# Attention in a streaming encoder step: the sink as one more column of the exponential, and the division by the sums placed behind the other unit's split

## The chip, the cores and the metric

The kernel is one program for one core of a Trainium2 chip. A NeuronCore has five engines that run their own instruction streams in order: TensorE (PE: matmuls, with the weight loads drawn as a row of their own, PEld), VectorE (DVE), ScalarE (ACT), GpSimd (POOL) and SyncE (SP, which only issues DMAs here). The metric is the device time of one launch, in microseconds; a comparison uses the median of several runs.

## The reference, cut to what matters

The reference is one inference step of an encoder with two layers: a recurrent layer (RG-LRU), then shared keys and values, then a layer of sliding-window attention with 16 heads in 4 groups, each group sharing one key/value head. 1024 prompt rows and 32 sample rows go through it. The change concerns the softmax, which has one learnt number per head, the sink, as an extra candidate that takes weight and gives no value:

```python
def sink_softmax(s, sink):
    m = jnp.maximum(jnp.max(s, axis=-1, keepdims=True), sink)
    p = jnp.exp(s - m)
    return p / (jnp.sum(p, axis=-1, keepdims=True) + jnp.exp(sink - m))
...
    p = sink_softmax(s, sink)
    o = jnp.einsum('bnkgqs,bnskd->bnqkgd', p.astype(vb.dtype), vb)
```

A block of 128 query rows sees at most 256 keys: its own block and the one before, masked in chunks of 64.

## The kernel before

The recurrent layer, the key/value projections and the queries of group 0 fill the first part of the program (lines 92 to 987). Every fp32 product is made of three matmuls: a helper `split` (lines 112 to 117) rounds an operand to a high half on ScalarE (L116) and subtracts to get the low half on VectorE (L117), and TensorE multiplies high by high, high by low and low by high.

The attention is the loop at lines 1058 to 1076. It runs over four groups g and, in each, over nine units j: eight blocks of 128 prompt rows and one of the sample rows, 36 units in all. A unit has three stages:

- `stage_s` (lines 903 to 941): the scores S of four heads (one for the sample unit) by two matmuls each (L925) into PSUM banks that are two deep; on VectorE one fused instruction per head adds the mask, scales, writes the negated scores into the unit's tile P and gives the row's extreme against the negated sink into `sm` (L927, followed by a read of the accumulator); on ScalarE the exponential of each head in place, with the row sum as a second result (L930). Then the sink's share: VectorE adds sink and extreme (L932), ScalarE takes the exponential of those four numbers (L933), VectorE adds it to the sums (L934) and takes the reciprocal (L935). Last the division: heads 2 and 3 on ScalarE (L938), heads 0 and 1 on VectorE (L940). P is two deep.
- `stage_t` (lines 943 to 952): TensorE transposes the powers of each of the (up to) two key blocks into PSUM banks T, two deep (L949), and `split` makes the halves ph on ScalarE and pl on VectorE.
- `stage_o` (lines 954 to 968): the output matmuls with ph and pl against the packed values (L959) into a single PSUM bank O, which ScalarE and VectorE then empty (L961, L967).

The loop issues the scores of unit j+1 first, then the transposes and split of unit j, then some steps of `fillers` (other matmuls that need no attention result: the gate projection `gB`, the next group's query projection `rAq`/`rBq`, and in the last group the first output projection `obm`), then the output matmuls of unit j. So a unit's transposes stand one round behind its scores, with the fillers between.

What is written so is not yet the order on the engines. The framework's scheduler reorders the instructions of each engine by a timeline that it simulates itself; `urgent()` raises the priority of what stands inside it, and `pin(i)` (line 79) keeps an instruction behind what the program issues ahead of it. All engines then run the order in which the scheduler left them. Lines 824 to 827 load the sinks into a tile `snk` and make their negatives `nsnk`.

Of the kernel before, what the change touches and what calls it, by code (L numbers as in the profile page):

```python
# [9 lines left out]
F32 = mybir.dt.float32  # L10
F32R = mybir.dt.float32r
AF = mybir.ActivationFunctionType
ALU = mybir.AluOpType
# [4 lines left out]
P = 128  # L18
# [45 lines left out]
def _trunk(ctx, tc, nc, A):  # L64
    V, S, G = nc.vector, nc.scalar, nc.gpsimd
# [13 lines left out]
    def pin(i, on=True):  # L79
        return tc.keep_in_program_order(i) if on else i  # L80

    def bank(name, tag="mm", bufs=None):
        return psum.tile([P, 512], F32, tag=tag, name=name, bufs=bufs or nbank)
# [28 lines left out]
    def split(dst_hi, dst_lo, src, lo_eng=None, hi_dve=False, behind=False):  # L112
        if hi_dve:
            V.tensor_copy(dst_hi, src)
        else:
            pin(S.activation(dst_hi, src, AF.Copy), behind)  # L116
        (lo_eng or V).tensor_tensor(dst_lo, src, dst_hi.bitcast(F32), op=ALU.subtract)  # L117
# [444 lines left out]
    for n in range(3):  # L562
        for m in LATE:
            w = NSB[n][1] - NSB[n][0]
# [87 lines left out]
    for n, order in enumerate(orders):  # L652
        zs, acc = {}, []
        w = NSB[n][1] - NSB[n][0]
# [25 lines left out]
    def att_tile(name, shape, dt, tag, bufs):  # L680
        return att.tile([P] + shape, dt, tag=tag, bufs=bufs, name=name)

    def kv_tile(name, shape, dt, tag, bufs=1):
        return kvp.tile([P] + shape, dt, tag=tag, bufs=bufs, name=name)
# [38 lines left out]
    def run(gen):  # L723
        for _ in gen:
            pass
# [95 lines left out]
    smask = kv_tile("smask", [256], F32, "smask")  # L821
    V.memset(smask, 0.0)
    V.memset(smask[:, 160:], NEG)
    snk = kv_tile("snk", [20], F32, "snk")
    nsnk = kv_tile("nsnk", [20], F32, "nsnk")
    nc.scalar.dma_start(snk, A["snk"])
    V.tensor_scalar(nsnk, snk, -1.0, None, op0=ALU.mult)

    prep_v()
    for n in range(3):  # L830
# [37 lines left out]
    ON_ACT = (2, 3)  # L868
# [5 lines left out]
    def load_kv(g, n):  # L874
        KU[g, n] = att_tile(f"K{g}_{n}", [2, 640], F32R, "K", 2)
        VU[g, n] = att_tile(f"V{g}_{n}", [5, 128], F32R, "V", 2)
        w = KB1[n] - KB0[n]
        for dup in range(2):
            for half in range(2):
                p0 = dup * 64 + half * 32  # L880
                pin(nc.sync.dma_start(KU[g, n][p0:p0 + 32, :, :w].bitcast(F32),
                                      kscr.rearrange("(l f) p c -> p l f c", l=2)[32 * g:32 * g + 32, :, half, KB0[n]:KB1[n]]),
                    g == 0 and n > 0)
        t0, t1 = KB0[n] // P, KB1[n] // P
        nc.sync.dma_start(VU[g, n][:, :t1 - t0, :].bitcast(F32),
                            vscr.rearrange("t p c -> p t c")[:, t0:t1, g * 128:g * 128 + 128])
# [16 lines left out]
    def stage_s(g, j):  # L903

        smp = j == 8
        n = 2 if smp else j // 3
        if (g, n) not in KU:
            load_kv(g, n)
        nm = f"{g}_{j}"
        nh, nk = (1 if smp else 4), (1 if j == 0 else 2)  # L910
        t0 = 3 if smp else max(j - 1, 0) - KB0[n] // P
        w = nk * P
        ks = slice(t0 * P, t0 * P + 256)
        sm = att_tile(f"sm{nm}", [4, 4], F32, "sm", 4)
        nmax, d, rsum, rl = (sm[:, i, :nh] for i in range(4))
        sk = slice(16 + g, 17 + g) if smp else slice(4 * g, 4 * g + 4)
        msk = smask if smp else mask[:, 256 - w:]
        pt = att_tile(f"P{nm}", [4, 256], F32, "P", 2)
        for h0 in range(0, nh, 2):
            sb = bank(f"S{nm}_{h0}", "S", 2)  # L920
            for h in range(h0, min(h0 + 2, nh)):
                q = QS[g].rearrange("p h c -> p (h c)") if smp else QU[g, n][:, h, P * j - NSB[n][0]:P * j - NSB[n][0] + P]
                s = sb[:, (h - h0) * 256:(h - h0) * 256 + 256]
                for hl in range(2):
                    pin(nc.tensor.matmul(s, q, KU[g, n][:, hl, ks], start=hl == 0, stop=hl == 1), g == 0 and j == 0)  # L925
            for h in range(h0, min(h0 + 2, nh)):
                V.tensor_tensor_reduce(pt[:, h, :w], sb[:, (h - h0) * 256:(h - h0) * 256 + w], msk,  # L927
                                       -0.125, nsnk[:, sk][:, h:h + 1], op0=ALU.add, op1=ALU.min,
                                       accum_out=nmax[:, h:h + 1])
                S.activation(pt[:, h, :w], pt[:, h, :w], AF.Exp, bias=nmax[:, h:h + 1], scale=-1.0,  # L930
                             accum_out=rsum[:, h:h + 1])
        V.tensor_tensor(d, snk[:, sk], nmax, op=ALU.add)  # L932
        S.activation(d, d, AF.Exp)  # L933
        V.tensor_tensor(rsum, rsum, d, op=ALU.add)  # L934
        V.reciprocal(rl, rsum)  # L935
        for h in range(nh):
            if h in ON_ACT:
                S.activation(pt[:, h, :w], pt[:, h, :w], AF.Copy, scale=rl[:, h:h + 1])  # L938
            else:
                V.tensor_scalar(pt[:, h, :w], pt[:, h, :w], rl[:, h:h + 1], None, op0=ALU.mult)  # L940
        return dict(P=pt, nh=nh, nk=nk, t0=t0, n=n, nm=nm, smp=smp)

    def stage_t(st):
        nm, w = st["nm"], st["nh"] * P
        st["p"] = []
        for kt in range(st["nk"]):
            tb = bank(f"T{nm}_{kt}", "T", 2)[:, :w]
            for h in range(st["nh"]):
                nc.tensor.transpose(tb[:, h * P:(h + 1) * P], st["P"][:, h, kt * P:(kt + 1) * P], ident)  # L949
            hl = [att_tile(f"p{x}{nm}_{kt}", [512], F32R, "p" + x, 2)[:, :w] for x in "hl"]  # L950
            split(*hl, tb)
            st["p"].append(hl)

    def stage_o(g, j, st):
        n, w, nk = st["n"], st["nh"] * P, st["nk"]
        ob = bank(f"O{st['nm']}", "O", 1)[:, :w]
        for kt in range(nk):
            for i, x in enumerate(st["p"][kt]):
                nc.tensor.matmul(ob, VU[g, n][:, st["t0"] + kt, :], x, start=kt + i == 0, stop=kt == nk - 1 and i == 1)  # L959
        half = kv_tile(f"oh{st['nm']}", [512], F32, "oh")  # L960
        S.activation(half[:64, :w], ob[64:128], AF.Copy)  # L961
        q = w // 4
        c0 = 256 if st["smp"] else P * j - NSB[n][0]
        if (g, n) not in TT:
            TT[g, n] = [unit(f"T{g}_{n}_{i}", w=NSB[n][1] - NSB[n][0]) for i in range(2)]
        for h in range(4):
            V.tensor_tensor(TT[g, n][h // 2][64 * (h % 2):64 * (h % 2) + 64, c0:c0 + q],  # L967
                            ob[:64, h * q:(h + 1) * q], half[:64, h * q:(h + 1) * q], op=ALU.add)
# [3 lines left out]
    def finish_og(g, n):  # L972
        for i in range(2):
            t, m = TT[g, n][i], 2 * g + i
            V.scalar_tensor_tensor(t, t, 0.5, SG.pop((m, n)), op0=ALU.mult, op1=ALU.mult)
            if g < 3:
                nc.scalar.dma_start(ogscr[m][:, NSB[n][0]:NSB[n][1]], t)
            else:
                ogl[m, n] = t
        del TT[g, n]  # L980
# [8 lines left out]
    def fillers(g):  # L989
        for m in (2 * g, 2 * g + 1):  # L990
            prep_m(f"g{m}", A["w_in_b"][8 + m], KD, 3)
        for n in range(3):
            for m in (2 * g, 2 * g + 1):
                yield from gate_block(m, n)
            if g == 3:
                for m in OG_AT[n]:
                    load_og(m, 0)
        for m in (2 * g, 2 * g + 1):
            del wts[f"g{m}"]
        if g < 3:  # L1000
            for x, nm in enumerate("AB"):
                prep_m(f"q{nm}{g + 1}", A["w_in_b"][2 * (g + 1) + x], KD, 3)
            for n in range(3):
                yield from q_block(g + 1, n)
        else:
            yield from out_b(0)
# [51 lines left out]
    for g in range(4):  # L1058
        fil = fillers(g)
        per = PER[g]  # L1060
        todo = [0, 1, 2]
        st = {0: stage_s(g, 0)}
        for j in range(9):
            if j < 8:
                st[j + 1] = stage_s(g, j + 1)
            stage_t(st[j])
            for _ in range(per - (g == 3 and j > 6)):
                next(fil, None)
            stage_o(g, j, st.pop(j))
            while todo and j >= (2, 5, 8)[todo[0]] and (2 * g + 1, todo[0]) in SG:  # L1070
                finish_og(g, todo.pop(0))
        if g == 3:
            break
        run(fil)
        for n in todo:
            finish_og(g, n)
# [164 lines left out]
```

## Time and profile before

| what | before |
|---|---|
| median of the timed runs | 914.59 us (914.43, 914.59, 915.57) |
| the profiled execution, its own time | 918.22 us |
| its span, first to last instruction | 916.4 us |
| granted TensorE clock, mean over the span | 0.993 |
| stretch of the attention in the span | about 548 to 845 us |

The span is what the trace covers; the execution's own time is 1.8 us longer. The profile is of another execution than the timed ones and lies 3.6 us above their median, so terms taken from it are set off against its own time. In a row of groups the columns are: line, engine, operation, tile written <- tiles read, shapes, count | busy time and mean ns of one | idle time of that engine just before, and what ended it. A row of waits names the engine and line that waited, what it waited for, the total in us, how often, and the longest.

### The profile page before, as it was taken

How to read it: one execution, taken by the hardware profiler on the slowest of the kernel's cores; microseconds unless marked ns; L12 is line 12 of the kernel's file. 1: busy time of each engine (PE TensorE's matmuls, PEld its weight loads, DVE VectorE, ACT ScalarE, POOL GpSimd, SP SyncE). 2: the span in 40 equal slices, each digit the busy share in tenths (PEclk: the TensorE clock that was granted, in tenths of full speed). 3: DMA queues.
4: the chain of work that ended last, by engine and by line, in shares of the span. 5: the costliest groups of instructions: out<-in, count | busy, mean ns of one | idle time of the engine just before them, and what ended most of it. 6: DMA issues, size and time to landing. Idle time of an engine off the chain costs nothing.

```text
span 916.4 us, 15897 instructions
## 1 busy us (share of the span) xinstructions
PE 891.0 (97%) x5434; PEld 864.6 (94%) x5434; DVE 721.5 (79%) x1571; ACT 562.8 (61%) x1231; POOL 212.5 (23%) x263
## 2 busy tenths in 40 slices
PE   9989999999999999999999999999999999899997
PEld 8989999999999999999989899999999998889985
DVE  5796878878897663185987758999989998898686
ACT  8747877869453334364663327666666766797661
POOL 5240222114300001124354521122212111202130
PEclk9989999999999999999999999999999999999999
DMA  9532433342543325445556586256347346424884
GB/s 336 197 84 67 134 94 118 93 123 88 174 134 118 89 83 163 133 145 183 161 173 191 167 235 155 95 158 184 96 131 212 95 118 183 136 96 137 288 268 160
DMA packets 95778, 137.35 MB, mean 150 GB/s; under 512 B 16145, under 2 KB 64305, under 8 KB 95697
## 3 DMA queue, kind: packets, MB, share of 16 engines
q1 hardware_dynamic: 86040, 123.30, 44.4%
q10 hardware_dynamic: 9480, 12.49, 4.4%
q8 instruction: 43, 0.70, 0.3%
q0 software_dynamic: 176, 0.54, 0.2%
q14 instruction: 39, 0.31, 0.1%
HBM read 99.28 MB, written 32.13 MB: 143 GB/s over the span
## 4 chain that ended last, share of the span: by engine, by line
PE 62%; DVE 19%; DMA 4%; ACT 3%; issue 3%; SPq 1%; POOL 1%; DVEq 0%; ACTq 0%; POOLq 0%
PE gb L151 5%; PE gb L152 5%; PE gb L150 5%; PE obm L698 4%; PE gB L698 4%; PE oa L151 4%; PE oa L150 4%; PE oa L152 4%; PE br L151 3%; PE br L150 3%; PE br L152 3%; PE ot L698 2%; DVE T L967 2%; DVE pl L117 2%; DVE P L927 2%
## 5 line engine op out<-in xcount | busy, mean ns | idle before, releaser
L150 PE MATMUL oa<-yh,whi_outa 128*128 128x384 f32 (+1 forms) x264 | 85.8, 325 | 0.0
L151 PE MATMUL gb<-xlo,whi_ina 128*128 128x384 f32 (+1 forms) x264 | 85.5, 324 | 0.0
L152 PE MATMUL gb<-xhi,wlo_ina 128*128 128x384 f32 (+1 forms) x264 | 85.3, 323 | 0.0
L150 PE MATMUL gb<-xhi,whi_ina 128*128 128x384 f32 (+1 forms) x264 | 85.1, 322 | 0.0
L151 PE MATMUL oa<-yl,whi_outa 128*128 128x384 f32 (+1 forms) x264 | 85.1, 323 | 0.0
L152 PE MATMUL oa<-yh,wlo_outa 128*128 128x384 f32 (+1 forms) x264 | 85.0, 323 | 0.0
L930 ACT ACTIVATE P<-P,sm 128x256 f32<-128x256 f32 (+1 forms) x132 | 64.0, 486 | 26.4 <-DVE sm L927 26.1
L150 PE MATMUL br<-xhi,whi_ina 128*128 128x384 f32 (+1 forms) x240 | 78.4, 327 | 0.0
L151 PE MATMUL br<-xlo,whi_ina 128*128 128x384 f32 (+1 forms) x240 | 78.4, 326 | 0.0
L152 PE MATMUL br<-xhi,wlo_ina 128*128 128x384 f32 (+1 forms) x240 | 77.8, 325 | 0.0
L117 DVE TENSOR_TENSOR wlo_outa<-raw_outa,whi_outa 128x512 fp32r<-128x512 f32 (+1 forms) x60 | 43.7, 741 | 42.0 <-ACT whi_outa L116 41.9
L616 POOL TENSOR_TENSOR qp<-qp,qp 128x384 f32<-128x384 f32 (+2 forms) x34 | 39.2, 1154 | 149.4 <-ACT qp L614 137.5
L698 PE MATMUL gB<-xh,whi_g 128*128 128x384 f32 (+1 forms) x192 | 63.2, 329 | 0.0
L698 PE MATMUL gB<-xh,wlo_g 128*128 128x384 f32 (+1 forms) x192 | 63.1, 329 | 0.0
L698 PE MATMUL gB<-xl,whi_g 128*128 128x384 f32 (+1 forms) x192 | 62.9, 328 | 0.0
L116 ACT ACTIVATE whi_outa<-raw_outa 128x512 fp32r<-128x512 f32 (+1 forms) x60 | 35.4, 594 | 41.9 <-PE oa L151 24.3
L224 DVE SCALAR_TENSOR_TENSOR conv<-ext,pa,conv 128x1060 f32<-128x1060 f32 (+2 forms) x51 | 50.1, 1005 | 9.0 <-ACT conv L222 8.6
L927 DVE CUSTOM_DVE_ANT_0 P<-S,mask,nsnk 128x256 f32<-128x256 f32 (+1 forms) x128 | 52.8, 461 | 0.1
L150 PEld LDWEIGHTS oa<-yh,whi_outa 128*128 128x128 f32 x264 | 49.6, 188 | 0.4
L151 PEld LDWEIGHTS oa<-yl,whi_outa 128*128 128x128 f32 x264 | 49.5, 188 | 0.4
L152 PEld LDWEIGHTS oa<-yh,wlo_outa 128*128 128x128 f32 x264 | 49.6, 188 | 0.0
L150 PEld LDWEIGHTS gb<-xhi,whi_ina 128*128 128x128 f32 x264 | 49.6, 188 | 0.0
(303 smaller groups left out, 2913.2 us busy)
## 6 DMA issues: line engine op xcount, KB each, us to landing
raw_ina<-w_in_a SPq DMA_DIRECT2D x44, 256.0 KB, 2.9
raw_outa<-w_out_a SPq DMA_DIRECT2D x40, 256.0 KB, 2.6
raw_ob<-w_out_b SPq DMA_DIRECT2D x32, 256.0 KB, 2.7
qscr<-quadq SPq DMA_DIRECT2D x8, 768.0 KB
Q<-qscr SPq DMA_DIRECT2D x32, 192.0 KB, 5.2
hscr<-u SPq DMA_DIRECT2D x11, 530.0 KB, 3.3
xr<-xr SPq DMA_DIRECT2D x8, 512.0 KB, 10.3
raw_g<-w_in_b SPq DMA_DIRECT2D x16, 256.0 KB, 2.6
```

What stands on the lines that cost most here:

```text
L116: pin(S.activation(dst_hi, src, AF.Copy), behind)
L117: (lo_eng or V).tensor_tensor(dst_lo, src, dst_hi.bitcast(F32), op=ALU.subtract)
L150: nc.tensor.matmul(ps, wh, xh, start=i == 0, stop=False)
L151: nc.tensor.matmul(ps, wh, xl, start=False, stop=False)
L152: nc.tensor.matmul(ps, wl, xh, start=False, stop=last and i == n - 1)
L224: V.scalar_tensor_tensor(c, e[:, c0 + k:c1 + k], pa[:, t, k:k + 1], c, op0=ALU.mult, op1=ALU.add)
L616: G.tensor_tensor(sums[0], sums[0], q, op=ALU.add)
L698: nc.tensor.matmul(ps, l, r, start=c == 0, stop=c == 3 * n - 1)
L927: V.tensor_tensor_reduce(pt[:, h, :w], sb[:, (h - h0) * 256:(h - h0) * 256 + w], msk, -0.125, nsnk[:, sk][:, h:h + 1], op0=ALU.add, op1=AL ...
L930: S.activation(pt[:, h, :w], pt[:, h, :w], AF.Exp, bias=nmax[:, h:h + 1], scale=-1.0, accum_out=rsum[:, h:h + 1])
L967: V.tensor_tensor(TT[g, n][h // 2][64 * (h % 2):64 * (h % 2) + 64, c0:c0 + q], ob[:64, h * q:(h + 1) * q], half[:64, h * q:(h + 1) * q], o ...
```

## The change

The negated sink is copied by ScalarE into one more column of the tile P, one column per head (new line 919), and the exponential of each head then runs over that column too (w + 1 columns), so that its row sum already holds the sink's share. The two small additions and the small exponential are gone, and with them the tile `snk`: the sinks are loaded straight into `nsnk` and negated in place. P has rows of 258 instead of 256 numbers, `sm` three rows instead of four.

The reciprocal and the division move out of `stage_s` into a stage of their own, `stage_n`, which the loop calls for unit j+1 behind the split of unit j; for a group's first unit it is called right behind the scores. The first of the two divisions on ScalarE is pinned there, so the scheduler may not take it ahead of the other unit's split.

```diff
-    snk = kv_tile("snk", [20], F32, "snk")
     nsnk = kv_tile("nsnk", [20], F32, "nsnk")
-    nc.scalar.dma_start(snk, A["snk"])
-    V.tensor_scalar(nsnk, snk, -1.0, None, op0=ALU.mult)
+    nc.scalar.dma_start(nsnk, A["snk"])
+    V.tensor_scalar(nsnk, nsnk, -1.0, None, op0=ALU.mult)
...
-        pt = att_tile(f"P{nm}", [4, 256], F32, "P", 2)
+        pt = att_tile(f"P{nm}", [4, 258], F32, "P", 2)
+        S.activation(pt[:, :nh, w:w + 1], nsnk[:, sk].unsqueeze(2), AF.Copy)
...
-                S.activation(pt[:, h, :w], pt[:, h, :w], AF.Exp, bias=nmax[:, h:h + 1], scale=-1.0,
+                S.activation(pt[:, h, :w + 1], pt[:, h, :w + 1], AF.Exp, bias=nmax[:, h:h + 1], scale=-1.0,
                              accum_out=rsum[:, h:h + 1])
-        V.tensor_tensor(d, snk[:, sk], nmax, op=ALU.add)
-        S.activation(d, d, AF.Exp)
-        V.tensor_tensor(rsum, rsum, d, op=ALU.add)
-        V.reciprocal(rl, rsum)
-        for h in range(nh):
+        return dict(P=pt, nh=nh, nk=nk, t0=t0, n=n, nm=nm, smp=smp, w=w, rsum=rsum, rl=rl)
+
+    def stage_n(st, behind=True):
+
+        pt, w, rl = st["P"], st["w"], st["rl"]
+        V.reciprocal(rl, st["rsum"])
+        for h in range(st["nh"]):
             if h in ON_ACT:
-                S.activation(pt[:, h, :w], pt[:, h, :w], AF.Copy, scale=rl[:, h:h + 1])
+                pin(S.activation(pt[:, h, :w], pt[:, h, :w], AF.Copy, scale=rl[:, h:h + 1]), behind and h == ON_ACT[0])
             else:
                 V.tensor_scalar(pt[:, h, :w], pt[:, h, :w], rl[:, h:h + 1], None, op0=ALU.mult)
-        return dict(P=pt, nh=nh, nk=nk, t0=t0, n=n, nm=nm, smp=smp)
...
         st = {0: stage_s(g, 0)}
+        stage_n(st[0], False)
         for j in range(9):
             if j < 8:
                 st[j + 1] = stage_s(g, j + 1)
             stage_t(st[j])
+            if j < 8:
+                stage_n(st[j + 1])
```

What the scheduler makes of it on ScalarE is shown at unit 0_5 (group 0, block 5), beside the split of unit 0_4. P0_5 is the unit's tile of powers, sm0_5 its sums, ph0_4_0 and ph0_4_1 the high halves of the other unit's transposed powers T0_4, oh0_4 the copy of half of an output bank. Before:

```order
L930 ACTIVATE P0_5_6671,sm0_5_6670<-P0_5_6671,sm0_5_6670 128x256 x4
L933 ACTIVATE sm0_5_6670<-sm0_5_6670 128x4
L938 ACTIVATE P0_5_6671<-P0_5_6671,sm0_5_6670 128x256 x2
L116 ACTIVATE ph0_4_0_6703<-T0_4_0_6698 128x512
L116 ACTIVATE ph0_4_1_6712<-T0_4_1_6707 128x512
```

And now:

```order
L931 ACTIVATE P0_5_6660,sm0_5_6659<-P0_5_6660,sm0_5_6659 128x257 x2
L116 ACTIVATE ph0_4_0_6685<-T0_4_0_6680 128x512
L931 ACTIVATE P0_5_6660,sm0_5_6659<-P0_5_6660,sm0_5_6659 128x257
L116 ACTIVATE ph0_4_1_6694<-T0_4_1_6689 128x512
L931 ACTIVATE P0_5_6660,sm0_5_6659<-P0_5_6660,sm0_5_6659 128x257
L919 ACTIVATE P0_6_6788<-nsnk_5312 128x4
L941 ACTIVATE P0_5_6660<-P0_5_6660,sm0_5_6659 128x256 x2
```

The two splits have moved from behind the division to places among the exponentials, the small exponential is gone, and the next unit's copy of the sink stands ahead of the division.

The same place on VectorE; pl0_4_0 and pl0_4_1 are the low halves, rp0q1_0 a product of the rotary embedding for the next group's queries. Before:

```order
L932 TENSOR_TENSOR sm0_5_6670<-snk_5312,sm0_5_6670 128x4
L715 TENSOR_TENSOR rp0q1_0_6858<-rAq1_0_6744,cos_3707 128x384
L934 TENSOR_TENSOR sm0_5_6670<-sm0_5_6670 128x4
L935 RECIPROCAL sm0_5_6670<-sm0_5_6670 128x4
L940 TENSOR_SCALAR P0_5_6671<-P0_5_6671,sm0_5_6670 128x256 x2
L117 TENSOR_TENSOR pl0_4_0_6704<-T0_4_0_6698,ph0_4_0_6703 128x512
L117 TENSOR_TENSOR pl0_4_1_6713<-T0_4_1_6707,ph0_4_1_6712 128x512
```

And now:

```order
L117 TENSOR_TENSOR pl0_4_0_6686<-T0_4_0_6680,ph0_4_0_6685 128x512
L117 TENSOR_TENSOR pl0_4_1_6695<-T0_4_1_6689,ph0_4_1_6694 128x512
L938 RECIPROCAL sm0_5_6659<-sm0_5_6659 128x4
L715 TENSOR_TENSOR rp0q1_0_6843<-rAq1_0_6731,cos_3707 128x384
L943 TENSOR_SCALAR P0_5_6660<-P0_5_6660,sm0_5_6659 128x256 x2
```

The low halves have moved ahead of the reciprocal and the division, and the two additions are gone. In other units, such as 0_3 and 3_3, reciprocal and division still stand ahead of the low halves on VectorE, where nothing is pinned. TensorE's order is made anew too: the transposes of a unit's two key blocks now mostly stand side by side, and the fillers between a unit's stages are dealt out more evenly. On SP the loads of the values move up by a few places at four points and two weight loads by one or two.

More of the change, by code (lines that the diff above doesn't have):

```diff
@@ L913, in stage_s @@
         ks = slice(t0 * P, t0 * P + 256)
-        sm = att_tile(f"sm{nm}", [4, 4], F32, "sm", 4)
-        nmax, d, rsum, rl = (sm[:, i, :nh] for i in range(4))
+        sm = att_tile(f"sm{nm}", [3, 4], F32, "sm", 4)
+        nmax, rsum, rl = (sm[:, i, :nh] for i in range(3))
         sk = slice(16 + g, 17 + g) if smp else slice(4 * g, 4 * g + 4)
         msk = smask if smp else mask[:, 256 - w:]
-        pt = att_tile(f"P{nm}", [4, 256], F32, "P", 2)
+        pt = att_tile(f"P{nm}", [4, 258], F32, "P", 2)
+        S.activation(pt[:, :nh, w:w + 1], nsnk[:, sk].unsqueeze(2), AF.Copy)
         for h0 in range(0, nh, 2):
```

## The prediction

> **What bounds the kernel now.** The profile's first part says what kind of kernel this is.
>
> ```profile
> span 916.4 us, 15897 instructions
> PE 891.0 (97%) x5434; PEld 864.6 (94%) x5434; DVE 721.5 (79%) x1571; ACT 562.8 (61%) x1231; POOL 212.5 (23%) x263
> ```
>
> TensorE's matmul row is busy 97% of the span, so what a change in another engine can give is limited to the time in which TensorE has nothing to do. The edits sit in the attention, from its first score matmul (L925) to its last output matmul (L959); the views of these two lines give its ends, near 548 and 845 us.
>
> ```profile
> L925 PEld LDWEIGHTS S<-K,Q x256: 186/188/193, 547.9 to 810.6; 128*128 128x128 f32 x128
> L959 PE MATMUL O<-pl,V x68: 273/393/504, 562.1 to 844.9; 128*128 128x512 f32 x60, 128*128 128x128 f32 x8
> ```
>
> The windows view, asked for 548 to 848:
>
> ```profile
> core 0: us, PE busy (x) PEld busy (x) DVE busy (x) ACT busy (x) POOL busy (x), PEclk, DMA share, GB/s
> 548.00:848.00 300.00, 292.08 (x1864) 278.35 (x1863) 270.57 (x834) 210.05 (x589) 59.33 (x55) 1.00 0.49 139
> ```
>
> Over 300 us TensorE is busy 292.08, VectorE 270.57 (90%), ScalarE 210.05 (70%), and the granted clock is full. TensorE's idle time by this row, 7.92 us, is too small, as one stretch shows, which is also the stretch to follow the change through. First TensorE, at a wait for the high half of unit 0_4's powers (unit g_j is group g, query block j).
>
> ```profile
> 592.25 0.34 PE L698 MATMUL rBq<-xh,whi_qB 128*128 128x384 f32 x1
> 592.42 0.34 PE L698 MATMUL rBq<-xl,whi_qB 128*128 128x384 f32 x1
> 593.12 0.34 PE L698 MATMUL rBq<-xh,wlo_qB 128*128 128x384 f32 x1
> 593.90 0.19 PEld L959 LDWEIGHTS O<-ph,V 128*128 128x128 f32 x1 [0.77 <-ACT ph L116]
> 593.90 0.50 PE L959 MATMUL O<-ph,V 128*128 128x512 f32 x1 [0.45 <-ACT ph L116]
> ```
>
> Matmuls of 384 columns start every 0.17 us but are drawn 0.34 long, so the first 0.17 of a wait is painted as busy; the pause from 593.12 to 593.90 is 0.45 in the matmul row and 0.77 in the row of weight loads. I therefore take the waits of the weight loads as the list of what TensorE loses in 548 to 848.
>
> ```profile
> PEld S L925 <- DVE sm L927: 2.4, 4, 1.6
> PEld O L959 <- DVE pl L117: 2.3, 5, 0.8
> PEld T L949 <- DVE pl L117: 1.6, 1, 1.6
> PEld O L959 <- ACT ph L116: 1.3, 2, 0.8
> PEld O L959 <- ACT sm L933: 1.3, 1, 1.3
> PEld T L949 <- DVE P L940: 1.1, 2, 0.6
> PEld O L959 <- ACT whi_g L116: 1.0, 1, 1.0
> PEld O L959 <- ACT quadq L116: 0.9, 1, 0.9
> PEld obm L698 <- ACT ogh L116: 0.8, 1, 0.8
> PEld T L949 <- issue: 0.3, 1, 0.3
> PEld obm L698 <- DVE ogl L117: 0.3, 1, 0.3
> PEld O L959 <- ACT sg L896: 0.2, 1, 0.2
> ```
>
> The rows add up to 13.5 us, in waits of at most 1.6 us each. This is the cap: nothing that the change does to VectorE or ScalarE can give more. [...] By the matmul row the cap would be 7.9 and the forecast below, scaled, 3.7 us instead of 6.4.
>
> Now ScalarE and VectorE in the same stretch.
>
> ```profile
> 590.96 0.20 ACT L933 ACTIVATE sm<-sm 128x4 f32<-128x4 f32 x1 [0.60 <-DVE sm L932]
> 592.32 0.91 ACT L938 ACTIVATE P<-P,sm 128x256 f32<-128x256 f32 x2 [1.15 <-DVE sm L935]
> 593.25 1.09 ACT L116 ACTIVATE ph<-T 128x512 fp32r<-128x512 f32 x2
> 590.77 0.16 DVE L932 TENSOR_TENSOR sm<-snk,sm 128x4 f32<-128x4 f32 x1
> 590.85 0.55 DVE L715 TENSOR_TENSOR rp0q<-rAq,cos 128x384 f32<-128x384 f32 x1
> 591.32 0.70 DVE L934 TENSOR_TENSOR sm<-sm 128x4 f32<-128x4 f32 x1
> 592.05 0.18 DVE L935 RECIPROCAL sm<-sm 128x4 f32<-128x4 f32 x1
> 592.26 0.62 DVE L940 TENSOR_SCALAR P<-P,sm 128x256 f32<-128x256 f32 x2
> ```
>
> Unit 0_5's sums walk VectorE, ScalarE, VectorE (590.77 to 592.05); ScalarE stands 0.60 and 1.15 us for that walk, divides unit 0_5 for 0.91, and only then splits unit 0_4's transposed powers, for which TensorE waits. Unit 0_5's own transposes come later.
>
> **The change part by part.** The groups it touches, all in 548 to 848:
>
> ```profile
> L930 ACT ACTIVATE P<-P,sm 128x256 f32<-128x256 f32 (+1 forms) x132 | 64.0, 486 | 26.4 <-DVE sm L927 26.1
> L932 DVE TENSOR_TENSOR sm<-snk,sm 128x4 f32<-128x4 f32 (+1 forms) x36 | 7.9, 220 | 0.5
> L933 ACT ACTIVATE sm<-sm 128x4 f32<-128x4 f32 (+1 forms) x36 | 7.0, 194 | 1.4 <-DVE sm L932 1.2
> L934 DVE TENSOR_TENSOR sm<-sm 128x4 f32<-128x4 f32 (+1 forms) x36 | 9.5, 263 | 5.8 <-ACT sm L933 5.7
> L938 ACT ACTIVATE P<-P,sm 128x256 f32<-128x256 f32 (+1 forms) x64 | 28.1, 487 | 18.1 <-DVE sm L935 18.1
> L940 DVE TENSOR_SCALAR P<-P,sm 128x256 f32<-128x256 f32 (+1 forms) x68 | 25.4, 410 | 0.7
> ```
>
> *Removed on VectorE:* 72 small adds (L932, L934). As busy time they are 7.9 + 9.5 = 17.4 us; as issue room each is worth 0.08 us (the next instruction starts at 590.85, 0.08 after 590.77), together 5.8. I take 5.8, because the rest overlaps the neighbours, and keep 17.4 as the other end. The wait of L934 for ScalarE's small exponential, 5.7 us, goes too: nothing of the sink is left to wait for. VectorE is relieved by 11.5 us; its idle time of 300 - 270.57 = 29.4 would become 40.9.
>
> *ScalarE:* 36 small exponentials (194 ns each) go and 36 small copies of the negated sink come. No copy of four elements is in the trace; between nothing (it may fill an idle place; the buffer it writes is free, since it stands behind the splits that wait for that buffer's last readers) and twice the exponential I take the same 194, so zero net, ±7.0 us on an engine with 90 us idle in this window. The exponentials get one column more out of 257; at 486 ns for 256 that is at most 2 ns each, 0.3 us over 132, on ScalarE. [...]
>
> *Row pitch 258 instead of 256 and the sink loaded straight into its negated tile:* nothing; the same elements move, and the sink's sign change lies 200 us ahead of its use:
>
> ```profile
> L827 DVE TENSOR_SCALAR nsnk<-snk x1: 177/177/177, 347.8 to 347.8; 128x20 f32<-128x20 f32 x1
> ```
>
> *The division moved.* On ScalarE the first division of a unit is pinned behind the other unit's split, so the 18.1 us in which ScalarE stood with a division at its head, waiting for a reciprocal, no longer hold up a split. What is queued behind the new waiting instruction is the next unit's exponentials; who waits for them is the next reciprocal, not TensorE directly. TensorE's order is remade as well (the scheduler places all of it again), with the two transposed halves of a unit side by side and the output matmuls later.
>
> *What of TensorE's 13.5 us goes.* I sort the list by what stood directly ahead. (a) Held by the removed steps or by a division standing ahead of a split: O for ph 1.3, O behind L933 1.3, T for pl 1.6 (there too a division stands right ahead of the split on VectorE), T for P 1.1; 5.3 us, all of it gone. (b) Held by VectorE or ScalarE being late in general: S for L927 2.4, O for pl 2.3, whi_g 1.0, quadq 0.9; 6.6 us. I let these shrink in proportion to VectorE's slack, 11.5 of 40.9, so 28% or 1.9 us. (c) The rest, 1.6 us, belongs to the output projection and stays. (d) A remade order makes waits of its own; bounds are nothing and a few of the largest now seen (1.6); I take half of one, 0.8. Sum: 5.3 + 1.9 - 0.8 = 6.4 us. The tail behind 848 follows unchanged, only earlier.
>
> The profiled execution took 918.22 us, 1.8 more than its span of 916.4; 918.22 - 6.4 = 911.8. The three timed runs have their median at 914.59, 3.6 below the profiled one, so I forecast 914.59 - 6.4 = **908.2 us**. A measurement of this kernel can tell about 0.2%, 1.8 us, from no change.
>
> **The rivals.**
> *All of it goes:* (a) and (b) vanish, 11.9 us, 902.7. For it: every wait of (a) and (b) hangs on the two engines that are relieved. Against it: VectorE stays at about 86% busy, and S for L927 waits for work that the change doesn't touch. Chance 0.18.
> *Moved, not removed:* TensorE works in order, so a wait that ends earlier only meets the next late operand. For it: the pin holds on ScalarE alone. Counted in the order, the reciprocal still stands ahead of the other unit's pl on VectorE in 13 of 32 units (17 before). Gain under 1.8, about 914. Chance 0.14.
> *The division comes too late:* if a split waits for its transposes, the division pinned behind it waits too, with its sums ready, and the next transposes are late. Price: the two splits in front, 1.09 us per unit. It can only happen where TensorE has less than four exponentials, two splits and two divisions between a unit's scores and its transposes (4 × 0.49 + 1.09 + 0.91 = 4.0 us); with 36 matmuls of 0.17 in between, 6.1 us, most units are safe, and those at a group's edges and in the last group are not. Seven units paying it eat up (a) and (b); at nine the kernel is slower, 914.59 + 9 × 1.09 - 7.2 = 917.2. Chance 0.10.
> That the scheduler ignores the pin is excluded by the order; on ScalarE the splits do stand ahead.
>
> **How the numbers follow.** The forecast case (gain 1.8 to 9) has 0.58. Faster by over 0.2%: 0.58 + 0.18 = 0.76; within: 0.14; slower: 0.10. The range runs from 902.5 (all of it) to 915.5 (moved, not removed, with a little loss); it leaves out the slower rival and a case in which 17.4 rather than 5.8 us of VectorE's time matters.
>
> **What would show it.** In the profile after: no waits on L932 to L934 rows; ScalarE's wait in front of its divisions shrinks from 18.1 us or no longer has a split behind it; the weight loads' waits in the attention add up to 5 to 9 us instead of 13.5; VectorE's busy time falls by 10 to 17 us. If those waits fall and the time doesn't, the tail has eaten it; if O for ph and T for P are still there, the order argument is wrong; if T for P grows past 1.1 us, the late-division rival is right.

## The result, and the profile after

The changed kernel takes 904.68 us (median of 903.07, 903.56, 905.81 and 906.49) against 914.99 for the kernel before (914.43 to 915.57, four runs): ratio 0.9879, 95% interval 0.9858 to 0.9900. That is 10.3 us where 6.4 were forecast, and 3.5 us under the forecast time.

The first lines of the page of after:

```profile
span 904.0 us, 15787 instructions
PE 885.4 (98%) x5434; PEld 864.4 (96%) x5434; DVE 708.1 (78%) x1499; ACT 563.1 (62%) x1231; POOL 221.7 (25%) x263
```

TensorE issues the same 5434 matmuls. VectorE has 72 instructions fewer and is busy 13.4 us less. The two lines that bound the attention, now L926 (scores) and L961 (output):

```profile
L926 PEld LDWEIGHTS S<-K,Q x256: 187/188/193, 546.2 to 805.4; 128*128 128x128 f32 x128
L961 PE MATMUL O<-pl,V x68: 219/394/482, 559.7 to 828.9; 128*128 128x512 f32 x60, 128*128 128x128 f32 x8
```

From the first score to the start of the last output matmul it is now 828.9 - 546.2 = 282.7 us, before 844.9 - 547.9 = 297.0: the attention is 14.3 us shorter. The stretch ahead of it is 1.7 shorter; TensorE's order in it is the same, and over the traces of all the kernels its end lies anywhere between 544.9 and 547.9, so this is scatter of the execution. The stretch behind it is longer: 904.0 - 828.9 = 75.1 against 71.5, so 3.6 us are given back. Together 14.3 + 1.7 - 3.6 = 12.4, the difference of the two spans (916.4 - 904.0); the medians differ by 10.3, because the profiled execution of before lay 3.2 above the median of 914.99 and that of after 1.1 above its own.

The border between these two stretches has moved too. The windows view of the attention, before and after:

```profile
547.90:844.90 297.00, 289.08 (x1848) 275.39 (x1847) 267.56 (x828) 207.53 (x584) 57.92 (x54) 1.00 0.50 140
546.20:828.90 282.70, 282.31 (x1838) 275.00 (x1836) 253.49 (x755) 205.46 (x579) 56.94 (x53) 1.00 0.49 146
```

Ten matmuls of the output projection (obm), which start 0.19 us apart, now stand behind the last output matmul instead of ahead of it. So 1.9 of the 14.3 us, and 1.9 of the 3.6, are work that changed sides.

The same window, 548 to 848, with TensorE, weight loads, VectorE, ScalarE and GpSimd in this order:

```profile
548.00:848.00 300.00, 299.41 (x1922) 291.22 (x1922) 264.26 (x775) 217.11 (x602) 58.69 (x54) 1.00 0.51 154
```

TensorE's row has gone from 292.08 to 299.41 and holds 58 matmuls more. What is left of its 13.5 us of waits, between 548 and 845:

```profile
PEld T L951 <- ACT P L941: 0.7, 2, 0.5
PEld obm L698 <- DVE ogl L117: 0.6, 1, 0.6
PEld T L951 <- DVE P L943: 0.4, 1, 0.4
PEld O L961 <- DVE pl L117: 0.2, 1, 0.2
```

These are 1.9 us: nearly everything went, not half of it. The 0.6 at obm comes near 835, behind the attention, so inside the attention 1.3 us are left and 12.2 went; with the 1.9 of work that changed sides this is 14.1 of the 14.3 us. The timeline of after at the place that the prediction walked through (a unit's split in the first group, its division behind it; idle time ahead in brackets):

```profile
584.82 0.60 ACT L116 ACTIVATE ph<-T 128x512 fp32r<-128x512 f32 x1
585.81 0.59 ACT L116 ACTIVATE ph<-T 128x512 fp32r<-128x512 f32 x1
586.98 1.28 DVE L117 TENSOR_TENSOR pl<-T,ph 128x512 fp32r<-128x512 f32 x2
588.17 0.17 DVE L938 RECIPROCAL sm<-sm 128x4 f32<-128x4 f32 x1
588.38 0.91 ACT L941 ACTIVATE P<-P,sm 128x256 f32<-128x256 f32 x2 [1.40 <-DVE sm L938]
588.88 0.19 PEld L698 LDWEIGHTS rBq<-xh,wlo_qB 128*128 128x128 f32 x1
589.05 0.19 PEld L961 LDWEIGHTS O<-ph,V 128*128 128x128 f32 x1
```

Both high halves are done at 586.40, the low ones at 588.26, and TensorE loads the first of them at 589.05, 0.17 us behind the last filler, without a wait (before: 0.77). ScalarE still stands 1.40 us for the reciprocal, but no split that TensorE waits for is behind it. Over the whole attention, by groups:

```profile
L931 ACT ACTIVATE P<-P,sm 128x257 f32<-128x257 f32 (+1 forms) x132 | 64.3, 490 | 8.0 <-DVE sm L928 7.9
L941 ACT ACTIVATE P<-P,sm 128x256 f32<-128x256 f32 (+1 forms) x64 | 29.0, 491 | 13.2 <-DVE sm L938 11.7 <-DVE P L943 0.6 <-DVE T L977 0.6
L919 ACT ACTIVATE P<-nsnk 128x4 f32<-128x4 f32 (+1 forms) x34 | 7.0, 205 | 0.0
```

ScalarE's waits ahead of the exponentials fell from 26.1 to 7.9 and those ahead of its divisions from 18.1 to 11.7. The copy of the sink takes 205 ns (194 were taken), the longer exponential 490 (486 before, 488 expected).

The longest wait of the tail, from the timeline of after:

```profile
874.05 0.48 PEld L1125 LDWEIGHTS xt<-ident,x1t 128*128 128x128 f32 x3
874.65 0.63 ACT L116 ACTIVATE wthi<-raw_t 128x512 fp32r<-128x512 f32 x1 [0.86 <-DMA raw_t<-w_out_t]
875.18 0.50 ACT L614 ACTIVATE qp<-obm 128x416 f32<-128x416 f32 x1
875.82 1.10 POOL L616 TENSOR_TENSOR qp<-qp,qp 128x416 f32<-128x416 f32 x1 [2.85 <-ACT qp L614]
876.97 0.30 PEld L158 LDWEIGHTS ss_p<-qp,ones 128*128 128x128 f32 x2 [2.44 <-POOL qp L616]
878.06 0.34 PEld L698 LDWEIGHTS ot<-wtl,ogh 128*128 128x128 f32 x1 [0.35 <-issue]
878.49 0.33 PEld L698 LDWEIGHTS ot<-wth,ogl 128*128 128x128 f32 x1
```

ScalarE stands for a weight's DMA with the split of that weight at its head (0.86 us here, and 0.79 and 1.42 at two more such waits up to 870.67); behind it stands the last square of the second output projection, behind that GpSimd's last add, and for the add TensorE waits 2.44 us (before 0.2). Then its matmuls start 0.43 us apart instead of 0.23 for a while, and the windows view of after has the granted clock of that stretch, third from the right, at 0.87 (before, it was 1.00 there):

```profile
870.00:880.00 10.00, 7.79 (x30) 5.77 (x29) 6.58 (x12) 7.09 (x14) 2.22 (x2) 0.87 0.73 229
```

The tail of before had a wait of its own, which after doesn't meet:

```profile
PEld ot L698 <- ACT zb L1043: 1.6, 1, 1.6
```

By the times between the starts of TensorE's matmuls in the two traces, the 3.6 us are made up of 1.9 for the ten matmuls, 2.3 for the wait at ss_p and 1.5 for the lower clock, less 2.1 for this wait and smaller ones among the matmuls of obm. So the tail by itself lost 1.7 us. This is one execution; whether the others of this kernel show the same wait is not known.

### The profile page after: what moved, and what is told of

The parts are those of the page before. It is cut to its first block, busy times and chain, and to the rows that moved or that the text cites. A ratio compares the mean times of both kernels' runs of the same rounds, so it can differ in the third digit from the quotient of the medians.

```text
span 904.0 us, 15787 instructions
## 1 busy us (share of the span) xinstructions
PE 885.4 (98%) x5434; PEld 864.4 (96%) x5434; DVE 708.1 (78%) x1499; ACT 563.1 (62%) x1231; POOL 221.7 (25%) x263
## 5 line engine op out<-in xcount | busy, mean ns | idle before, releaser
L616 POOL TENSOR_TENSOR qp<-qp,qp 128x384 f32<-128x384 f32 (+2 forms) x34 | 49.3, 1449 | 138.2 <-ACT qp L614 126.5
L931 ACT ACTIVATE P<-P,sm 128x257 f32<-128x257 f32 (+1 forms) x132 | 64.3, 490 | 8.0 <-DVE sm L928 7.9
```

The lines of the kernel that those rows point to most:

```text
L616: G.tensor_tensor(sums[0], sums[0], q, op=ALU.add)
L931: S.activation(pt[:, h, :w + 1], pt[:, h, :w + 1], AF.Exp, bias=nmax[:, h:h + 1], scale=-1.0, accum_out=rsum[:, h:h + 1])
```

## The experiments

Three readings of the gain were set against each other. *The walk:* VectorE waits, with its whole queue behind it, for a small result that has to come back from ScalarE (5.7 us in sum at L934 before). *The load:* the two adds for each unit take VectorE's time (220 and 263 ns each before, by their busy time). *The order:* the division stands ahead of the other unit's split. All kernels were timed in five rounds against before; gains in us are (1 - ratio) × 915, and the interval of each ratio is ±0.0018 to ±0.0027, so about ±2 us. By this rule the changed kernel gains 11.1; its medians differ by 10.3, because the ratio isn't the quotient of the two medians.

**The column alone.** The changed kernel with the division back in its old place:

```diff
                 st[j + 1] = stage_s(g, j + 1)
+                stage_n(st[j + 1], False)
             stage_t(st[j])
-            if j < 8:
-                stage_n(st[j + 1])
```

> The changed kernel with reciprocal and division back where they were, right behind the scores of the same unit; the sink stays a column of the exponential. Theory L (load and walk): most of the 10.3 us come from the 72 small adds, the small exponential and the waits between them that are gone; then this kernel keeps 7 us or more of the gain, 908 us or less, and the weight loads' waits in the attention stay under 5 us. Theory P (place): most comes from the division standing behind the other unit's split; then this kernel gains 4 us at most, 911 us or more, with O waiting for ph and pl again.

Measured: 902.37 us, ratio 0.9872 (0.9845 to 0.9899), gain 11.7. The column gives all of it, within the noise. TensorE's waits in 548 to 845:

```profile
PEld S L926 <- DVE sm L928: 0.5, 1, 0.5
PEld T L951 <- ACT P L941: 0.5, 1, 0.5
PEld obm L698 <- ACT ogh L116: 0.2, 1, 0.2
```

With the division called where it was, the waits for ph and pl, which I had put down to that place, are gone.

**The move alone.** The kernel before, with L934, the reciprocal and the division in the new place:

```diff
-        V.tensor_tensor(rsum, rsum, d, op=ALU.add)
-        V.reciprocal(rl, rsum)
...
+    def stage_n(st, behind=True):
+        V.tensor_tensor(rsum, rsum, st["d"], op=ALU.add)
+        V.reciprocal(rl, rsum)
```

> The kernel before with the second add, the reciprocal and the division moved behind the other unit's split, pinned as in the change; the sink keeps its two adds and its small exponential. Theory L: gain of 3 us at most, 912 us or more. Theory P: gain of 6 to 9 us, 906 to 909 us, and no wait of O for ph is left. If both parts are worth their own waits, the gains of this kernel and of the column alone add up to about 10 us.

Measured: 910.03, ratio 0.9940 (0.9918 to 0.9963), gain 5.5. TensorE's waits in the same stretch:

```profile
PEld S L925 <- DVE sm L927: 1.6, 2, 1.3
PEld T L953 <- DVE P L945: 1.5, 3, 0.7
PEld obm L698 <- DVE ogl L117: 0.9, 2, 0.6
PEld O L963 <- DVE pl L117: 0.3, 1, 0.3
PEld T L953 <- ACT P L943: 0.2, 1, 0.2
```

These are 4.5 us. The move does cure the output matmuls (O for ph and pl, 3.6 before, 0.3 now); it leaves the scores and the transposes. The gain lies between the two theories (3 at most, 6 to 9), and theory P's sign, no O for ph, is there. So each part gains by itself, the column all and the move half, and the whole isn't the sum of the parts.

**No pin.** The changed kernel with `stage_n(st[j + 1], False)`.

> The changed kernel without the pin; the call stays behind the split, so that the scheduler alone decides. Theory P with the pin as its means: the scheduler takes divisions ahead of the last split again in 9 of 28 units, and 3 to 5 us are lost, 908 to 910 us. Theory L: within 1.5 us of the changed kernel, 903 to 906 us.

Measured: 906.55, ratio 0.9909 (0.9888 to 0.9930), gain 8.3. The waits in 548 to 845 are 2.7 us, all but 0.2 of them T for P. The time lies between the ranges of the two theories. The interval overlaps that of the changed kernel, so the pin isn't shown to be worth anything.

**Two adds put back as load.** Nobody reads what they write (`sm` gets its fourth row back for it):

```diff
+        for _ in range(2):
+            V.tensor_tensor(sm[:, 3, :nh], nsnk[:, sk], nmax, op=ALU.add)
         return dict(P=pt, nh=nh, nk=nk, t0=t0, n=n, nm=nm, smp=smp, w=w, rsum=rsum, rl=rl)
```

> The changed kernel with two small adds per unit put back on VectorE (sink plus extreme into a spare row that nobody reads), so that the load of the 72 adds is back and the walk between the engines is not. Theory L, if it is the load: 4 us or more are lost, 909 us or more. If it is the walk or the place: within 1.5 us of the changed kernel, 903 to 906 us.

Measured: 906.11, ratio 0.9901 (0.9876 to 0.9925), gain 9.1. TensorE's waits are 4.7 us:

```profile
PEld O L963 <- DVE pl L117: 3.2, 3, 1.1
PEld T L953 <- ACT P L943: 1.0, 1, 1.0
PEld obm L698 <- DVE ogl L117: 0.5, 1, 0.5
```

That is 0.1 us above the second theory's range and far from the first's 909. The load by itself brings a wait back; by the ratios it costs 2 us where 11 were at stake, and as the interval overlaps that of the changed kernel, even these 2 are not shown.

**The wait cut, the adds kept.** The kernel before; the sink's share is missing from the sums:

```diff
-        V.tensor_tensor(rsum, rsum, d, op=ALU.add)
+        V.tensor_tensor(rsum, rsum, nmax, op=ALU.add)
```

> The kernel before with one operand changed: the add that closed the sum of the row (line 934) reads the rows' minimum instead of the small exponential, so the sink's share is not in the sum; the small exponential is still computed and nothing reads it. All instructions, and so the load of VectorE and ScalarE, are those of before; only VectorE no longer waits for the small exponential. Theory A (the walk: VectorE to ScalarE and back to VectorE at the heads of both queues is what cost the time): most of the column's 12.7 us come back, 902.5 to 907. Theory B (the load: two adds on VectorE and one exponential on ScalarE for each unit): at most 2 us, 913 to 915. Between them, 907 to 913, each has a part, in proportion.

Measured: 907.50, ratio 0.9917 (0.9894 to 0.9939), gain 7.6; the waits are 5.3 us. This falls between the two theories: cutting the walk alone gains two thirds of what the column gains. But VectorE's own wait is still there. At the add it now waits for the exponentials themselves (before: 5.7 us, for ScalarE's L933), and in the changed kernel the reciprocal waits for them. The two rows, over the attention, from the groups of this run and from the waits of after:

```profile
L934 DVE TENSOR_TENSOR sm<-sm 128x4 f32<-128x4 f32 (+1 forms) x36 | 7.3, 203 | 5.3 <-ACT P L930 5.1
DVE sm L938 <- ACT P L931: 6.3, 9, 1.0
```

So what the cut gained isn't VectorE's idle time at that instruction. What did shrink are ScalarE's waits, ahead of the exponentials from 26.1 to 14.5 us and ahead of the divisions from 18.1 to 13.0.

**The walk put back, without the adds.** The column alone, with one more instruction on ScalarE:

```diff
+        S.activation(rsum, rsum, AF.Copy)
         return dict(P=pt, nh=nh, nk=nk, t0=t0, n=n, nm=nm, smp=smp, w=w, rsum=rsum, rl=rl)
```

> The column alone, with the walk put back by itself: behind the exponentials of a unit ScalarE copies the rows' sums in place, and VectorE's reciprocal waits for that copy, as its add waited for the small exponential before. VectorE gets no instruction more; ScalarE gets 36 of about 0.2 us. Theory A (the walk costs by itself, 7.6 us by the run that only cut it): 908 to 911 instead of 902.4. Theory B (the walk costs only together with VectorE's two adds, or what the run that cut it gained came from its other data): 902 to 905.

Measured: 907.57, ratio 0.9918 (0.9899 to 0.9938), gain 7.5: theory A's side, 0.4 us under its range. Putting the walk back costs 4.2 us by the ratios, where cutting it gained 7.6. TensorE's waits in 548 to 845:

```profile
PEld obm L698 <- ACT ogh L116: 2.5, 2, 1.4
PEld obm L698 <- DVE ogl L117: 1.4, 3, 0.6
PEld T L952 <- PE obm L698: 0.4, 1, 0.4
PEld S L926 <- DVE sm L928: 0.3, 1, 0.3
PEld O L962 <- DVE pl L117: 0.2, 1, 0.2
PEld T L952 <- ACT P L942: 0.2, 1, 0.2
```

They are 5.0 us, and most stand at a place that has nothing to do with the sums: the output projection's operands, which ScalarE and VectorE now split later.

**The same copy, with the division moved.** The added line is the same, in the changed kernel.

> The changed kernel with the same copy of the sums put back, so that the walk is there but the reciprocal stands behind the other unit's splits. If the move and the column are two cures of the same wait, the walk costs little here: 904.5 to 907, and 3 us or more less than in the run before. If the move hides nothing, it costs as much as there: 909 to 912.

Measured: 904.58, ratio 0.9876 (0.9859 to 0.9894), gain 11.3: the walk costs nothing that can be seen behind the move. The waits are 1.2 us:

```profile
PEld obm L698 <- DVE ogl L117: 0.5, 2, 0.3
PEld T L952 <- issue: 0.4, 1, 0.4
PEld T L952 <- ACT P L942: 0.3, 1, 0.3
```

**The wait cut and the division moved, the adds kept.** The move alone, with the sink's share missing:

```diff
-        V.tensor_tensor(rsum, rsum, st["d"], op=ALU.add)
+        V.tensor_tensor(rsum, rsum, st["nmax"], op=ALU.add)
```

> The move alone (add, reciprocal and division behind the other unit's split, sink still outside the exponential) with the add reading the rows' minimum instead of the small exponential, so the sink's share is not in the sum; all instructions stay, only the wait for the small exponential goes. It asks what is left between the move alone (910.0) and the changed kernel (904.7). Theory A (VectorE's two adds, since with the move the walk costs nothing): the same as the move alone, 909 to 911. Theory B (the walk is still paid in part behind the move, because the adds leave VectorE less room): 905 to 907.5.

Measured: 905.71, ratio 0.9880 (0.9853 to 0.9907), gain 11.0, and waits of 2.9 us. This is theory B's range and not theory A's: with the wait cut, the adds cost nothing that can be seen behind the move in this kernel. The changed kernel with two adds put back, 906.11, stands in the same place (walk gone, adds there, division moved) and gained 9.1; the two intervals overlap.

The gains side by side, with TensorE's waits in 548 to 845 in brackets, all in us. ("Adds only" are the two kernels without the sink's share and, behind the semicolon, the changed kernel with two adds put back; "walk only" and "neither" have the sink in the exponential.)

| | walk and adds | adds only | walk only | neither |
|---|---|---|---|---|
| division in its old place | 0 (13.5) | 7.6 (5.3) | 7.5 (5.0) | 11.7 (1.2) |
| division moved | 5.5 (4.5) | 11.0 (2.9); 9.1 (4.7) | 11.3 (1.2) | 11.1 (1.9) |

Three things can be taken away: the walk, the adds, the division's old place. Any one of them gains 5.5 to 7.6 us, any two 9.1 to 11.7, and the third nothing more that can be seen. Single pairs of one and two overlap in their intervals (the wait cut, 0.9894 to 0.9939, against the wait cut and the division moved, 0.9853 to 0.9907), so the step is carried by all the pairs and the waits together, not by one pair.

A rival stands untested: no run holds the order of the instructions fixed. The scheduler makes a new order for every kernel; even in the run that changes one operand, TensorE's order leaves that of before at 556 us. So "old place" and "moved" say where the program calls the division, not where it runs. Counted in the traces of ScalarE, both divisions of a unit run ahead of the other unit's last split in 13 of 28 units before, in 9 with the column alone, without the pin and with the wait cut, in 7 with the walk put back, and in none or one with the pin; there, one of the two, presumably the one without a pin, still runs ahead in 7 to 13. The move alone changes nothing but the order and gains 5.5 us, so a part of what the cut wait or the missing adds gained can be the new order.

**The sink's copy on VectorE.**

```diff
-        S.activation(pt[:, :nh, w:w + 1], nsnk[:, sk].unsqueeze(2), AF.Copy)
+        V.tensor_copy(pt[:, :nh, w:w + 1], nsnk[:, sk].unsqueeze(2))
```

> The changed kernel with the 36 copies of the sink's column on VectorE instead of ScalarE. Two small adds for each unit cost 1.4 us (906.1 against 904.7), so one small copy for each unit should cost about 0.7 us by the load of VectorE: 905 to 906. If ScalarE's 205 ns for each copy are what delays the chain, 36 of them are 7.4 us of its time and the kernel would gain: 902 to 904. Forecast: within 1 us of the changed kernel.

Measured: 904.01, ratio 0.9880 (0.9858 to 0.9902), the same as the changed kernel. The two placings of the copy can't be told apart.

**The sum over the last squares asked for later**, in the changed kernel and in the column alone:

```diff
-    for _ in out_t():
-        next(nb, None)
+    for i, _ in enumerate(out_t()):
+        if i > 4:
+            next(nb, None)
```

> The changed kernel, with the sum over the last squares (line 158, ss_p) asked for 16 matmuls later in the last part, so that TensorE no longer stands 2.4 us for GpSimd's last add. Theory A (the changed kernel loses its last 2 to 3 us against the column alone in this wait and in the lower clock granted behind it): 901 to 902.8, the wait at ss_p under 0.5 us, the tail behind the last output matmul 71 to 72.5 us instead of 75.1. Theory B (the wait hides a later one, the weights or the last normalization bound the tail): 904 to 905.5, and a wait of about 2 us elsewhere behind 832.

> The column alone, with the same later sum over the last squares. There the wait at ss_p was 0.3 us already, so by theory A nothing is left to gain: 901.5 to 903, the same as the column alone (902.4). If the later sum is worth something by itself (another order of TensorE's last work), it would come in below 901.

Measured: 903.36 (ratio 0.9869, 0.9845 to 0.9893) and 902.12 (0.9853, 0.9829 to 0.9877). In the first, the waits behind 832 are these, and the wait at ss_p is gone:

```profile
PEld obm L698 <- DVE ogl L117: 0.5, 1, 0.5
PEld ot L698 <- issue: 0.3, 2, 0.2
```

Its tail is 902.3 - 830.9 = 71.4 us, as theory A had it, against 75.1. But its attention took 284.3 us (546.6 to 830.9) where the changed kernel's took 282.7, with the same instructions in the same order ahead of the tail, so most of the tail's gain is hidden in the scatter between executions, and the time falls between the two theories. The second kernel lies in the range given for it, 901.5 to 903. That the column alone with this edit is the fastest of all is not shown to be a difference: its interval overlaps that of the changed kernel.

## Why the prediction was right in its sign and too small

*What bounds the kernel.* Right. The waits of the weight loads were the list of what could be had, and 12.2 of its 13.5 us went. That the weight loads were taken for it, and not the matmul row, made a difference: by the matmul row the cap was 7.9 us, and the attention became 14.3 us shorter, 1.9 of them by the ten matmuls that changed sides. The cap by the weight loads held: with the 12.2 us of waits that leaves 0.2 us that stand in no row.

*The sum, term by term, in waits of the list.*

| term | forecast | measured |
|---|---|---|
| (a) held by the removed steps or by a division ahead of a split | 5.3 | 4.9 (T for P on VectorE keeps 0.4) |
| (b) held by VectorE or ScalarE being late in general | 1.9 of 6.6 | 6.4 (O for pl keeps 0.2) |
| (c) the output projection's waits | 0 of 1.6 | 1.6 (the 0.6 now at obm stands behind the attention) |
| (d) new waits of the remade order | -0.8 | -0.7 (T for P on ScalarE) |
| the tail | 0 | -3.6, of them 1.9 work that changed sides |

Of (c), only 1.1 us are rows of the output projection (obm); 0.3 of T for issue and 0.2 of O for sg were counted with them.

The step that failed is (b): "I let these shrink in proportion to VectorE's slack, 11.5 of 40.9, so 28% or 1.9 us." Here the waits did not shrink in proportion to slack. The run that only cuts the wait leaves all 72 adds in place, and by the same rule its 5.7 of 5.7 + 29.4 would take 16% of (b); its waits of that kind fell from 6.6 to 1.5, all of it O for pl. The table of gains shows the shape: one relief takes half or more, the second all that is left, the third nothing. The reading that fits is that the operands were late by a little at many places, each covered or not by the fillers in front of TensorE, so that a small relief on the chain of a unit puts most of them under cover at once. That the cover is what is being used up is argued from the shape; it wasn't measured by itself, and the remade order stands beside it as the other reading. That the time fell into the range is owed to the range's width: its lower end was set by the rival in which all of (b) goes, and in the list that is nearly what happened.

*(a), the attribution.* Its total came out, its reason half. I had taken the division's place ahead of the split as the cause of the waits for ph and pl; with the column alone the division is called in that place, the scheduler leaves it ahead of the other unit's last split in 9 of 28 units on ScalarE (13 before), and the reciprocal ahead of its first low half in 15 of 32 on VectorE (17 before), and these waits go all the same. This fits a place that matters only while the chain in front of it is long; it doesn't show it.

*"On ScalarE the splits do stand ahead"* holds for one of the two divisions, presumably the pinned one: in the profiled run of after, the other runs ahead of the last split in 7 of 28 units.

*VectorE's relief* was given as issue room 5.8 and wait 5.7, near equal, and the two runs with one of them taken away gained the same (7.5 and 7.6). But the wait didn't go: 6.3 us of it stand in after at the reciprocal, and 5.1 in the run that cuts the walk. So the relief that was measured is the adds' alone, and by its own rule, 5.8 of 35.2, (b) would have given 1.1 us instead of 1.9 and been further off. The far end of the range for the adds, 17.4 us, isn't needed.

*The tail* "follows unchanged, only earlier": wrong by 3.6 us, 1.9 of them work from the attention and 1.7 lost. The wait of 2.44 us at ss_p and the lower clock behind it cost 3.8 us, and 2.1 us of other waits went. Of the other runs, those with the division moved show that wait at 2.1 to 3.6 us (1.3 with the copy on VectorE), but so does the one that only cuts the wait of L934, with 3.0, where the division is in its old place; the column alone has 0.3, and with the walk put back 0.8. So it isn't the move as such, and what decides whether the last square meets that weight's DMA stays open.

*The rivals.* "All of it goes", 902.7 at 0.18, lies nearer to the result (2.0 us) than the forecast (3.5); its objection, that S for L927 waits for work the change doesn't touch, fell: that wait is no longer in the list. "The division comes too late" did not happen: T for P is 1.1 us in sum, what it was. "Moved, not removed" fell with the 12.2 us.

*The announced signs.* VectorE's busy time fell by 13.4 (10 to 17 announced), ScalarE's wait ahead of its divisions from 18.1 to 11.7 (shrinks), TensorE's waits to 1.9 (5 to 9 announced), which is the sign that was wrong and pointed at (b).

## What to carry to other kernels

Where TensorE loses its time in many short waits (here of at most 1.6 us), a relief on the chain that feeds it need not pay in proportion. Here the first paid half or more, the second took the rest and the third added nothing, so each part of a change has to be timed alone, and of this change the column would have done. Where a result walks through a small instruction from engine to engine, the walk is to be timed apart from the instruction: here cutting it, with every instruction kept but the order remade by the scheduler, was worth 7.6 us, although the engine that waited at its end stood idle there almost as long as before. And where a scheduler remakes the order, the order has to be counted in the trace before a gain is put down to a place in the program. And read the tail of the program too: here the last square stood behind splits that waited 0.79 to 1.42 us for their weights' DMA. And a border between two stretches says little until the work on either side of it is counted.

## What the runs showed of the hardware that was not expected

The lower clock in the tail doesn't follow from the length of TensorE's pause alone. Behind the pause of 2.44 us in the changed kernel the granted clock of 870 to 880 was 0.87, and with one of 2.4 us in the run with the wait cut and the division moved it was 0.89; with one of 2.51 us (up to 875.91) in the run with the copy put back behind the move it stayed at 1.00. Without the pin the pause was 3.57 us, up to 879.47, and the clock was 1.00 there and in 880 to 890. The windows of the three runs other than the changed kernel, in this order, the last with both windows:

```profile
870.00:880.00 10.00, 7.87 (x31) 5.83 (x30) 6.67 (x13) 7.11 (x14) 2.46 (x2) 0.89 0.81 249
870.00:880.00 10.00, 7.73 (x35) 5.91 (x34) 7.50 (x13) 6.65 (x14) 2.22 (x2) 1.00 0.77 228
870.00:880.00 10.00, 6.67 (x32) 5.14 (x30) 6.52 (x14) 6.88 (x14) 2.22 (x2) 1.00 0.80 241
880.00:890.00 10.00, 10.00 (x44) 8.00 (x43) 9.17 (x19) 1.29 (x3) 0.00 (x0) 1.00 0.66 202
```

Each is one execution of its kernel; what decides whether a lower clock follows a pause was not shown.
